# Rows of w and u as two bf16 parts, and column sums placed ahead of the rows, in an RWKV WKV kernel

## The chip, the cores and the metric

The kernel runs on one NeuronCore of a Trainium2 chip. The metric is the device time of one execution in microseconds (us): the median of seven runs for the kernel before. The core has a matrix engine (TensorE, PE in the profile, with its loads of weights shown as PEld), a vector engine (VectorE, DVE), an activation engine (ScalarE, ACT), a general engine (GpSimd, POOL), a queue engine that here issues most transfers (SyncE, SP), and 16 DMA engines that move data between device memory and on-chip memory. The engines run at the same time, each in its own program order, and wait for each other through semaphores.

## The reference

For 16 batches, 2048 time steps and 256 channels, a decayed softmax-like average of v runs over time. It keeps a numerator `aa`, a denominator `bb` and a running maximum `pp` for stability:

```
for t in range(seq_len):
    ww = u + kk                       # the current step, with bonus u
    qq = max(pp, ww)
    e1, e2 = exp(pp - qq), exp(ww - qq)
    output[b, t] = (e1 * aa + e2 * vv) / (e1 * bb + e2 + 1e-08)
    ww = pp - w + kk                  # as the reference has it; w is the decay
    qq = max(ww, kk)
    e1, e2 = exp(ww - qq), exp(kk - qq)
    aa, bb, pp = e1 * aa + e2 * vv, e1 * bb + e2, qq
```

All inputs and the output are float32. k, v and the output are 33.55 MB each; w and u are one row of 256 numbers (1 KB) each.

## The kernel before

**Tiles and slots.** Time is cut into 16 stretches of 128 steps, and the batches into 4 groups of 4. A tile n (there are NP = 64, with n = 4c + p for stretch c and group p) holds 128 time steps on the partitions and 4 batches times 256 channels along the free side: 128 x 1024 numbers, 512 KB in float32. The main loop handles one tile in each slot n. The first ten slots (LAG = 10, line 416) only take in tiles; from slot 10 on (line 437) a slot also finishes the output of tile n - 10 in its denominators and n - 11 in its numerators; a last loop (line 478) works off the 11 outputs that are left.

**What happens to one tile.** `load_k` and `load_v` (lines 61 and 65) bring k and v in; six buffers for k, five for v. `round_k` (line 173) copies k into the fp32r type on DVE. `logs` (line 178) makes the exponents in PSUM on PE in two kinds of matmuls: *rows* (line 184), four matmuls of 32 partitions each, which sit side by side in the array and multiply a coefficient matrix CO (time positions) with a matrix WU that holds w and u as rows, and *steps* (line 189), four matmuls of 128 partitions that add k with the matrices NLE and NLZ. `exps` (line 197) takes exponentials on ACT into a bf16 ring EZR. `times_v` (line 218) multiplies them by v on DVE. `sums` (line 237) adds up each tile's exponentials over time, eight narrow matmuls with 32 output columns each, into a bank MISC for the state that passes from one stretch of 128 steps to the next. `den` and `num` (lines 346 and 360) are the prefix sums of denominators and numerators on PE; `recip` (line 352) makes 1/denominator on ACT as a logarithm (line 355) and an exponential (line 357); `mult` (line 364) multiplies numerator by reciprocal on DVE; `store` (line 368) writes the output.

**The state.** After every fourth tile a chain of small work carries the state on: `copy_sums` (ACT, line 249), `turn` (PE), `state_logs` (ACT), `state_frames`, `state_scan` and `state_offsets` (POOL and DVE, lines 271 to 291), `state_weights` (ACT), `state_chain` (DVE), `turn_back` (PE), `inject` (DVE and DMAs of POOL) and `state_next` (POOL). A table `plan` (line 382) says in which slot, and at which named place of it, each part is issued. `state_offsets` runs on DVE for stretches 0, 1 and 15 and on POOL for the others.

**What sets the order.** Every instruction goes through `K`, which keeps the program's order on its engine. So the order of the calls in a slot is the order on each engine. PE's order in a slot from 10 on is: num of one half, den, `turn_back` if it is due, sums of the tile before (in even slots), num of the other half, rows and steps of the next tile, sums of the tile before (in odd slots), `turn` if it is due. ACT's order is: exponentials, logarithm, exponential of the reciprocal, with small work between. DVE's is: mult, `round_k` of tile n + 2, cast of v, mult, times_v. The numerators share one PSUM bank (NUMB), so the second num waits for the first mult; the denominators share one pair of banks (DENB), so a den waits for the logarithm that reads the one before; and the exponents of tile n + 1 use the banks that the exponentials of tile n have read (from slot 10 on, `half`, line 166).

**The queue of transfers.** SyncE issues nearly all loads and stores in program order. In a slot it issues the load of k of tile n + 6, a load of v, and the store of tile n - 11. In slots from 10 on, every fourth v goes through a POOL transfer that writes bf16.

**The start.** w and u are brought in by two small transfers of ACT's queue into `wuf` (lines 99 to 110); ACT copies `wuf` into WU in fp32r (line 412); the first rows follow. Ten matmuls of zeros (`idle_matmuls`, line 410) keep PE running meanwhile.

Of the kernel before, what the change touches and what calls it, by code (L numbers as in the profile page):

```python
# [7 lines left out]
F32 = mybir.dt.float32  # L8
F32R = mybir.dt.float32r
BF16 = mybir.dt.bfloat16  # L10
ALU = mybir.AluOpType
ACT = mybir.ActivationFunctionType
# [3 lines left out]
def kernel(  # L16
# [9 lines left out]
    K = tc.keep_in_program_order  # L26
    PE, DVE, SC, POOL, SP = nc.tensor, nc.vector, nc.scalar, nc.gpsimd, nc.sync

    B, T, Dm = k.shape
    HS = 64  # L30
    TC = 2 * HS
    NST = T // TC
    D = 2 * Dm
    NP = 4 * NST
    RING = 12
    AHEAD = 6
# [5 lines left out]
    consts = ctx.enter_context(tc.tile_pool(name="consts", bufs=1))  # L42
# [18 lines left out]
    def load_k(n, queue=SP):  # L61
        kr_of[n] = kpool.tile([128, 4, Dm], F32, tag="kr", name="kr")
        K(queue.dma_start(out=kr_of[n], in_=rows_of(k, n)))

    def load_v(n, queue=SP):
        if v_mode(n) == "dma":
            VB[n] = vbpool.tile([128, 4, Dm], BF16, tag="vb", name="vb")
            K(POOL.dma_start(out=VB[n], in_=rows_of(v, n)))
        else:
            vr_of[n] = vpool.tile([128, 4, Dm], F32, tag="vr", name="vr")  # L70
            K(queue.dma_start(out=vr_of[n], in_=rows_of(v, n)))
# [9 lines left out]
    def matrix(name, dt):  # L81
        return consts.tile([128, 128], dt, tag=name, name=name)

    def fill(ap, value):
        K(DVE.memset(ap.bitcast(F32) if ap.dtype == F32R else ap, value))

    GE, NE = ALU.is_ge, ALU.not_equal

    def select(ap, cmp, fill, base, cm, pattern):
        K(POOL.affine_select(out=ap, in_=ap, pattern=pattern, compare_op=cmp,  # L90
                             fill=fill, base=base, channel_multiplier=cm))

    M1, I1, Lx, COf = [matrix(x, F32) for x in ("M1", "I1", "Lx", "COf")]
    wuf = consts.tile([128, 2, Dm], F32, tag="wuf", name="wuf")
    CB_of = [consts.tile([128, 4, 128], BF16, tag=f"CB{j}", name=f"CB{j}") for j in range(2)]
    idle = CB_of[1].rearrange("p b x -> p (b x)")
    OH = consts.tile([128, 56], BF16, tag="OH", name="OH")
    Sel = consts.tile([128, 3, 2, 2, 4, 2], F32, tag="Sel", name="Sel")
    def load_row(eng, r, g0, x):
        K(eng.dma_start(out=wuf.rearrange("(g r) n d -> r g n d", r=32)[r, g0:4], in_=bass.AP(  # L100
            tensor=x.tensor, offset=x.offset, ap=[[0, 4 - g0], [0, 2], list(x.ap[0])])))

    K(POOL.memset(wuf[:, 0], 0.0))
    fill(wuf[:, 1], 0.0)
    fill(idle, 0.0)
    fill(M1, -1.0)
    fill(I1, 0.0)
    load_k(0)
    load_row(SC, 0, 0, w)
    load_row(SC, 1, 2, u)  # L110
    for n in range(1, AHEAD):
        load_k(n)
        load_v(n - 1)
    K(SC.preload_act_table_set("natural_log_exp_and_others"))
# [2 lines left out]
                    allow_small_or_imprecise_dtypes=True))  # L117
    select(M1, GE, 0.0, -1, -1, [[1, 128]])
    select(I1, NE, 1.0, 0, -1, [[1, 128]])
    for g in (2, 3):  # L120
        select(COf, NE, 1.0, -32 * g - 1, 1, [[0, 128]])

    NLE, NLZ, CO = matrix("NLE", F32R), matrix("NLZ", F32R), matrix("CO", F32R)
    K(DVE.tensor_scalar(NLE, M1, 0.5, None, ALU.add))
    for h in range(2):
        fill(NLE[HS * h:HS * h + HS, HS * (1 - h):HS * (2 - h)], 0.0)
    K(DVE.tensor_tensor(NLZ, NLE, I1, ALU.add))
    K(DVE.tensor_copy(CO, COf))  # L130
    fill(Lx, 1.0)
    fill(Sel, 0.0)
    fill(OH, 0.0)
    for h in range(2):
        fill(OH[HS * h:HS * h + HS, 24 + h:25 + h], 1.0)
        fill(OH[HS * h:HS * h + 1, 32 + h:33 + h], 1.0)
    for j, r in ((0, 0), (1, 8), (2, 64)):
        for h in range(2):
            select(Sel[:, j, h], NE, 1.0, -r - h, 1, [[-16, 2], [-2, 4], [-32, 2]])
    select(Lx, GE, 0.0, -1, -1, [[1, 128]])  # L140

    for h in range(2):
        select(Lx, NE, 1.0, -(HS * h + HS - 1), 1, [[0, 128]])
    WU = consts.tile([128, D], F32R, tag="WU", name="WU")
    mats = {"OH": OH, "Sel": Sel.rearrange("p a h n c i -> p (a h) n (c i)")}

    def out_matrices(*names):
# [18 lines left out]
    def half(n, z):  # L166
        j = (2 * n + z) % 3 if n < TURNS else z
        return PS[:, 2 * j:2 * j + 2, :]

    def ez(n):  # L170
        return EZR[:, :, n % RING]

    def round_k(n):
        km = consts.tile([128, 4, Dm], F32R, tag=f"km{n % 2}", name="km") if n < 2 else KM[n - 2]
        K(DVE.tensor_copy(km, kr_of.pop(n)))  # L175
        KM[n] = km

    def logs(n):
        km = KM[n].rearrange("p (i n) d -> p i (n d)", i=2)

        def rows(q):
            for i in range(2):
                g = 32 * (2 * q + i)
                K(PE.matmul(half(n, q)[:, i, :], CO[g:g + 32, :], WU[g:g + 32, :], start=True, stop=False,  # L184
                            tile_position=(g, 0), skip_group_check=True))

        def steps(q):
            for i in range(2):
                K(PE.matmul(half(n, q)[:, i, :], (NLE, NLZ)[q], km[:, i, :], start=False, stop=True,  # L189
                            skip_group_check=True))  # L190

        rows(0)
        rows(1)
        steps(0)
        steps(1)
# [41 lines left out]
    def sums(n):  # L237
        c, p = divmod(n, 4)
        t = MISC[:, 0:Dm]
        for o in range(2):  # L240
            x = 24 - 16 * o - 2 * p
            for j in range(4):
                q, i = divmod(j, 2)
                K(PE.matmul(t[32 * j:32 * j + 32, :], mats["OH"][:, x:x + 32],  # L244
                            ez(n)[:, 2 * q, i, Dm * o:Dm * o + Dm],
                            start=p == 0 and o == 0, stop=p == 3 and o == 1,
                            tile_position=(0, 32 * j), skip_group_check=True))
# [33 lines left out]

    def state_offsets(c):
        E = DVE if c in ON_DVE else POOL
        A, P, F = [x[c % 2] for x in (A_of, P_of, F_of)]
        out = A.rearrange("p h m -> p m h")
        Q = tiny.tile([128, 32, 2], F32, tag="Q", name="Q")
        K(E.tensor_tensor(Q, P[:, :, 0:2], F[:, :, 1:3], ALU.add))
        K(E.tensor_tensor(out[:, :, 0:2], Q, P[:, :, 1:3], ALU.subtract))
        K(E.tensor_single_scalar(out[:, :, 2:4], Q, CAP, op=ALU.min))
        K(E.tensor_single_scalar(out[:, :, 4:6], P[:, :, 1:3], -1.0, op=ALU.mult))  # L290
        K(E.tensor_copy(LL_of[(c + 1) % 2][:, 0, :, 0:1], P[:, :, 2:3]))

    def state_weights(c):
        G = tiny.tile([128, 6, 32], F32, tag="G", name="G")
# [57 lines left out]
    def recip(n, between=lambda: None):  # L352
        rd = rpool.tile([128, 2, D], F32, tag="rd", name="rd")
        for i in (slice(0, 1), slice(1, 2)) if n == NP - 1 else (slice(0, 2),):
            K(SC.activation(rd[:, i, :], DENB[:, i, :], ACT.Ln, scale=RS))  # L355
            between()
            K(SC.activation(rd[:, i, :], rd[:, i, :], ACT.Exp, scale=-1.0))  # L357
        RD[n] = rd

    def num(n, bank, i):  # L360
        for m, q in (("LN", 2), ("IdN", 3)):
            K(PE.matmul(bank, mats[m], ez(n)[:, q, i, :], start=q == 2, stop=q == 3, skip_group_check=True))  # L362

    def mult(n, bank, i):
        rd = RD[n]
        K(DVE.tensor_mul(rd[:, i, :], bank, rd[:, i, :]))  # L366
# [35 lines left out]
    def small_work(n, where):  # L402
        for f, c in later.pop((n, where), []):
            f(c)

    def idle_matmuls(n, bank):
        for _ in range(n):
            K(PE.matmul(bank, idle[:, 0:128], idle, start=True, stop=True, skip_group_check=True))

    idle_matmuls(10, MISC)  # L410
    round_k(0)
    K(SC.activation(WU, wuf.rearrange("p n d -> p (n d)"), ACT.Copy))  # L412
    logs(0)
    round_k(1)
    cast_v(0)
# [21 lines left out]
    for n in range(LAG, NP):  # L437

        q, qp = n - LAG, n - LAG - 1
        load(n + AHEAD)  # L440
        if qp >= 0:
            num(qp, NUMB, 0)
        den(q)
        small_work(n, "nums")

        if n % 2 == 0:
            sums(n - 1)
        exps(n)
        small_work(n, "act")
        recip(q, lambda: small_work(n, "recip"))  # L450
        if qp >= 0:
            mult(qp, NUMB, 0)
        small_work(n, "mid")
        if n + 2 < NP:
            round_k(n + 2)
        if n + 1 < NP:
            cast_v(n + 1)
        else:
            times_v(n)
        if qp >= 0:  # L460
            num(qp, NUMB, 1)
            mult(qp, NUMB, 1)
        small_work(n, "scan")
        if qp >= 0:
            store(qp)
        if n + 1 < NP:
            times_v(n)
            small_work(n, "chain")
            logs(n + 1)
        else:  # L470
            den(q + 1)
        if n % 2:
            sums(n - 1)
        small_work(n, "pe")
    sums(NP - 1)
    small_work(NP, "copy")
# [1 line left out]
    for n in range(NP, NP + LAG + 1):  # L478

        q, qp = n - LAG, n - LAG - 1  # L480
# [52 lines left out]
```

## Time and profile before

| | us |
|---|---|
| median of 7 runs (lowest to highest) | 292.58 (292.48 to 293.07) |
| profiled execution, its own time | 292.75 |
| its span | 291.04 |
| PE busy in the span | 269.8 (93%) |
| DVE busy | 256.7 (88%) |
| ACT busy | 257.1 (88%) |
| POOL busy | 118.5 (41%) |
| all 256 matmuls of the rows (line 184) | 33.8 |
| all 512 matmuls of the sums (line 244) | 25.6 |
| read from and written to device memory | 67.12 and 33.55 MB, 346 GB/s over the span |

The span is the stretch between the first and the last instruction that the profiler saw; the execution's own time has 1.71 us around it. Engine times overlap, so their shares don't add up to 100%. A matmul's duration contains its way through the array, and the next one starts before it ends; the distance of two starts tells more than a duration. The DMA share is the mean busy share of the 16 DMA engines; it can exceed 1, as packets of one engine overlap. In a timeline, "idle before <- releaser" is the time that the engine sat idle before an instruction, and what ended it. Where several instructions are merged, x tells how many.

### The profile page before, as it was taken

What the parts mean: (1) busy time and instruction counts of PE and PEld (TensorE: products, weight loads), DVE (VectorE), ACT (ScalarE), POOL (GpSimd) and SP (SyncE); (2) the same over time, 40 slices, a digit from 0 to 9 for tenths busy, and PEclk for the clock granted to TensorE, in tenths of its full rate; (3) what the DMA queues carried; (4) which work ended last, traced back from release to release, by engine and by line L of the source; (5) the groups of instructions that cost most, each with busy time, mean ns of one, the idle gap of its engine ahead of it and who ended that gap; (6) DMA issues with size and microseconds to landing.
All of it is one profiled execution on the core that took longest, in us unless ns stands there. A gap on an engine that the chain in (4) does not pass through costs nothing. (4 is left out here: it accounts for less than half of the span.)

```text
span 291.0 us, 4961 instructions
## 1 busy us (share of the span) xinstructions
PE 269.8 (93%) x1694; PEld 123.5 (42%) x1694; DVE 256.7 (88%) x441; ACT 257.1 (88%) x253; POOL 118.5 (41%) x219
## 2 busy tenths in 40 slices
PE   6799799999999999999999999999899999998881
PEld 1444354545344443544444443444354344434330
DVE  4399999999999989999999989998998989986753
ACT  1468579999999999999999999999899998999892
POOL 6000244354455555353445555353455545342200
PEclk9689999999999999999999999999999999999999
DMA  6999999999999999999999999999999999984686
GB/s 222 348 348 349 348 333 323 301 380 356 357 379 331 383 328 385 330 383 353 361 377 341 382 333 385 329 384 347 366 375 338 376 334 384 335 286 153 220 289 216
DMA packets 103516, 97.86 MB, mean 336 GB/s; under 512 B 4151, under 2 KB 103491, under 8 KB 103491
## 3 DMA queue, kind: packets, MB, share of 16 engines
q1 hardware_dynamic: 93744, 93.07, 94.7%
q0 software_dynamic: 9440, 4.20, 10.0%
q10 hardware_dynamic: 306, 0.27, 0.3%
q8 instruction: 13, 0.21, 0.3%
q14 instruction: 13, 0.10, 0.1%
HBM read 67.12 MB, written 33.55 MB: 346 GB/s over the span
## 5 line engine op out<-in xcount | busy, mean ns | idle before, releaser
L202 ACT ACTIVATE EZR<-PS 128x2048 bf16<-128x2048 f32 x54 | 100.9, 1868 | 5.3 <-PE PS L189 2.4
L366 DVE TENSOR_TENSOR rd<-PS,rd 128x512 f32<-128x512 f32 (+1 forms) x118 | 86.4, 734 | 13.0 <-PE PS L362 10.0
L220 DVE TENSOR_TENSOR EZR<-EZR,vb 128x2048 bf16<-128x2048 bf16 x64 | 77.5, 1211 | 4.8 <-ACT EZR L200 4.2
L339 POOL DMA_DIRECT2D EZR<-cb x64 | 38.5, 606 | 87.9 <-DVE cb L334 81.4
L357 ACT ACTIVATE rd<-rd 128x1024 f32<-128x1024 f32 (+1 forms) x65 | 68.0, 1046 | 1.2
L355 ACT ACTIVATE rd<-PS 128x1024 f32<-128x1024 f32 (+1 forms) x65 | 65.6, 1009 | 1.6 <-PE PS L349 1.5
L362 PE MATMUL PS<-EZR,LN 128*128 128x512 bf16 x128 | 49.1, 383 | 2.8 <-DVE rd L366 1.0
L175 DVE CAST km<-kr 128x1024 fp32r<-128x1024 f32 x64 | 44.7, 698 | 6.2 <-DMA kr<-in_k_dram 6.0
L189 PE MATMUL PS<-km,NLE 128*128 128x512 f32 x128 | 48.2, 459 | 1.2 <-DVE km L175 1.2
L362 PE MATMUL PS<-EZR,IdN 128*128 128x512 bf16 x128 | 48.4, 378 | 0.0
L189 PE MATMUL PS<-km,NLZ 128*128 128x512 f32 x128 | 41.0, 401 | 0.0
L349 PE MATMUL PS<-EZR,L 128*128 128x512 bf16 x128 | 38.0, 379 | 1.9 <-ACT rd L355 1.9
L349 PE MATMUL PS<-EZR,Id 128*128 128x512 bf16 x128 | 38.1, 379 | 0.0
L215 DVE CAST vb<-vr 128x1024 bf16<-128x1024 f32 x50 | 36.6, 732 | 0.9 <-DMA vr<-in_v_dram 0.9
L184 PE MATMUL PS<-WU,CO 32*128 32x512 f32 x256 | 33.8, 505 | 3.4 <-ACT WU L412 3.2
L275 POOL TENSOR_TENSOR F<-LL,LL 128x32 f32<-128x32 f32 x13 | 8.6, 662 | 50.5 <-ACT LL L266 50.5
L200 ACT ACTIVATE EZR<-PS 128x1024 bf16<-128x1024 f32 x20 | 19.4, 1021 | 9.2 <-PE PS L189 9.2
L189 PEld LDWEIGHTS PS<-km,NLZ 128*128 128x128 f32 x128 | 24.7, 193 | 6.2
L189 PEld LDWEIGHTS PS<-km,NLE 128*128 128x128 f32 x128 | 19.5, 192 | 17.4 <-issue 14.4
L184 PEld LDWEIGHTS PS<-WU,CO 32*128 32x128 f32 x256 | 12.9, 184 | 31.1 <-issue 13.8
L244 PE MATMUL PS<-EZR,OH 128*32 128x256 bf16 x512 | 25.6, 278 | 0.0
L362 PEld LDWEIGHTS <-LN 128*128 128x128 bf16 x128 | 12.7, 100 | 19.0 <-issue 15.0
(69 smaller groups left out, 219.4 us busy)
## 6 DMA issues: line engine op xcount, KB each, us to landing
kr<-in_k_dram SPq DMA_DIRECT2D x64, 512.0 KB, 9.0
out_dram<-rd SPq DMA_DIRECT2D x63, 512.0 KB, 8.2
vr<-in_v_dram SPq DMA_DIRECT2D x50, 512.0 KB, 9.0
vb<-in_v_dram POOLq DMA_DIRECT2D x14, 256.0 KB, 8.4
EZR<-cb POOLq DMA_DIRECT2D x64, 8.0 KB, 5.0
out_dram<-rd SPq DMA_DIRECT2D x2, 128.0 KB, 2.9
out_dram<-rd ACTq DMA_DIRECT2D x2, 128.0 KB, 3.2
wuf<-in_w_dram ACTq DMA_DIRECT2D x1, 8.0 KB
```

The source lines that it names most:

```text
L175: K(DVE.tensor_copy(km, kr_of.pop(n)))
L184: K(PE.matmul(half(n, q)[:, i, :], CO[g:g + 32, :], WU[g:g + 32, :], start=True, stop=False, tile_position=(g, 0), skip_group_check=True))
L189: K(PE.matmul(half(n, q)[:, i, :], (NLE, NLZ)[q], km[:, i, :], start=False, stop=True, skip_group_check=True))
L202: K(SC.activation(ez(n)[:, 0:2], PS[:, 0:4, :].rearrange("p (q i) x -> p q i x", q=2), ACT.Exp))
L215: K(DVE.tensor_copy(vb, vr))
L220: K(DVE.tensor_mul(ez(n)[:, 2:4], ez(n)[:, 0:2], vb.unsqueeze(1).broadcast_to([128, 2, 2, D])))
L339: K(POOL.dma_start(out=EZR[r:r + 1, 2 * q, r0:r0 + 4, :, :].rearrange("o p i (b x) -> o (p i b) x", b=4), in_=cb[x:x + 32, :]))
L349: K(PE.matmul(DENB[:, i, :], mats[m], ez(n)[:, q, i, :], start=q == 0, stop=q == 1, skip_group_check=True))
L355: K(SC.activation(rd[:, i, :], DENB[:, i, :], ACT.Ln, scale=RS))
L357: K(SC.activation(rd[:, i, :], rd[:, i, :], ACT.Exp, scale=-1.0))
L362: K(PE.matmul(bank, mats[m], ez(n)[:, q, i, :], start=q == 2, stop=q == 3, skip_group_check=True))
L366: K(DVE.tensor_mul(rd[:, i, :], bank, rd[:, i, :]))
```

## The change

- `wuf` becomes 128 x 256 instead of 128 x 2 x 256. Each row of w (u) is now written to two partitions, 16 apart, of every group of 32. From it comes WU in bf16 in two steps: ACT makes a bf16 copy WUH, then DVE computes WUH x Rest + wuf and rounds that to bf16. Rest is 0 on the first partition of a pair, so that it holds the row rounded to bf16, and -1 on the second, so that it holds what the rounding lost. Rest is made at the start by one select of POOL and one reduction of DVE. CO becomes bf16 and has its coefficients on both partitions, which takes four selects on POOL instead of two. The rows read WU twice along the free side (a broadcast) instead of reading two copies.
- The row of u is issued by SyncE, behind the loads of k(0) and k(1) and ahead of v(0); before, ACT's queue issued it behind w. The order of the other loads stays.
- From slot 10 on, the sums of the tile before are issued at one place in every slot: behind the second num and ahead of the rows. The call of `recip` moves to the same place in the text; it is ACT's alone, so ACT's order stays as it was, apart from the two small works that it calls between.
- In `state_offsets` the last two operations go to POOL for all stretches but the last; before, DVE had them for stretches 0 and 1.

```diff
-    wuf = consts.tile([128, 2, Dm], F32, tag="wuf", name="wuf")
+    wuf = consts.tile([128, Dm], F32, tag="wuf", name="wuf")
+    WUH = consts.tile([128, Dm], BF16, tag="WUH", name="WUH")
+    Rest4 = consts.tile([128, 4, 2], F32, tag="Rest4", name="Rest4")
+    Rest = consts.tile([128, 1], F32, tag="Rest", name="Rest")
...
     def load_row(eng, r, g0, x):
-        K(eng.dma_start(out=wuf.rearrange("(g r) n d -> r g n d", r=32)[r, g0:4], in_=bass.AP(
-            tensor=x.tensor, offset=x.offset, ap=[[0, 4 - g0], [0, 2], list(x.ap[0])])))
-
-    K(POOL.memset(wuf[:, 0], 0.0))
-    fill(wuf[:, 1], 0.0)
+        K(eng.dma_start(out=wuf.rearrange("(j r) d -> r j d", r=16)[r, 2 * g0:8], in_=bass.AP(
+            tensor=x.tensor, offset=x.offset, ap=[[0, 8 - 2 * g0], list(x.ap[0])])))
+
+    K(POOL.memset(wuf, 0.0))
...
     load_k(0)
     load_row(SC, 0, 0, w)
-    load_row(SC, 1, 2, u)
-    for n in range(1, AHEAD):
+    load_k(1)
+    load_row(SP, 1, 2, u)
+    load_v(0)
+    for n in range(2, AHEAD):
         load_k(n)
         load_v(n - 1)
...
-    for g in (2, 3):
-        select(COf, NE, 1.0, -32 * g - 1, 1, [[0, 128]])
+    for x in (65, 81, 97, 113):
+        select(COf, NE, 1.0, -x, 1, [[0, 128]])
...
-    NLE, NLZ, CO = matrix("NLE", F32R), matrix("NLZ", F32R), matrix("CO", F32R)
+    NLE, NLZ, CO = matrix("NLE", F32R), matrix("NLZ", F32R), matrix("CO", BF16)
...
+    fill(Rest4, 0.0)
...
+    select(Rest4, NE, -1.0, -16, 1, [[-32, 4], [-1, 2]])
...
-    WU = consts.tile([128, D], F32R, tag="WU", name="WU")
+    WU = consts.tile([128, Dm], BF16, tag="WU", name="WU")
...
-                K(PE.matmul(half(n, q)[:, i, :], CO[g:g + 32, :], WU[g:g + 32, :], start=True, stop=False,
+                K(PE.matmul(half(n, q)[:, i, :], CO[g:g + 32, :],
+                            WU[g:g + 32, :].unsqueeze(1).broadcast_to([32, 2, Dm]), start=True, stop=False,
                             tile_position=(g, 0), skip_group_check=True))
...
     def state_offsets(c):
         E = DVE if c in ON_DVE else POOL
+        E2 = POOL if c < NST - 1 else DVE
...
-        K(E.tensor_single_scalar(out[:, :, 4:6], P[:, :, 1:3], -1.0, op=ALU.mult))
-        K(E.tensor_copy(LL_of[(c + 1) % 2][:, 0, :, 0:1], P[:, :, 2:3]))
+        K(E2.tensor_single_scalar(out[:, :, 4:6], P[:, :, 1:3], -1.0, op=ALU.mult))
+        K(E2.tensor_copy(LL_of[(c + 1) % 2][:, 0, :, 0:1], P[:, :, 2:3]))
...
     idle_matmuls(10, MISC)
+    K(DVE.tensor_reduce(Rest, Rest4.rearrange("p g j -> p (g j)"), mybir.AxisListType.X, ALU.add))
     round_k(0)
-    K(SC.activation(WU, wuf.rearrange("p n d -> p (n d)"), ACT.Copy))
+    K(SC.activation(WUH, wuf, ACT.Copy))
+    K(DVE.scalar_tensor_tensor(WU, WUH, Rest, wuf, ALU.mult, ALU.add))
     logs(0)
...
         den(q)
         small_work(n, "nums")
-
-        if n % 2 == 0:
-            sums(n - 1)
         exps(n)
         small_work(n, "act")
-        recip(q, lambda: small_work(n, "recip"))
...
         if qp >= 0:
             num(qp, NUMB, 1)
+
+        sums(n - 1)
+        recip(q, lambda: small_work(n, "recip"))
+        if qp >= 0:
             mult(qp, NUMB, 1)
...
             den(q + 1)
-        if n % 2:
-            sums(n - 1)
         small_work(n, "pe")
     sums(NP - 1)
```

## The prediction

> **What bounds the kernel now.** I read four views: first the slices and stretches of the span, for the DMA share beside the engines; then the waits, split into two stretches; then the timeline of one late slot; last the drained end. The index n below is a slot (one pass of the loop, one tile of k and v); "rows", "steps" and "sums" are the matmuls of lines 184, 189 and 244.
>
> Stretches of the span (length, busy time of each engine, granted clock, DMA share, GB/s):
>
> ```profile
> 5.00:35.00 30.00, 24.87 (x153) 11.86 (x151) 23.42 (x49) 17.60 (x21) 1.41 (x4) 0.89 1.10 349
> 75.00:80.00 5.00, 4.77 (x34) 2.06 (x26) 4.54 (x11) 4.84 (x6) 1.48 (x4) 1.00 1.09 385
> 175.00:180.00 5.00, 4.76 (x32) 2.11 (x32) 4.93 (x11) 4.84 (x5) 2.44 (x4) 1.00 1.09 385
> 240.00:245.00 5.00, 4.41 (x26) 2.05 (x26) 4.93 (x11) 4.32 (x6) 1.52 (x3) 1.00 1.09 384
> 262.00:270.00 8.00, 7.03 (x50) 3.35 (x49) 5.07 (x17) 6.93 (x9) 1.57 (x4) 1.00 0.43 139
> ```
>
> The DMA share is 1.09 to 1.10 from 5 us to 245 us, and the rate does not move (349 GB/s while only loads run, 384 to 385 with stores among them) whether the engines are in their first, middle or late slots. It falls to 0.43 only after 262 us. So the transfers look full from the start until the last loads are in.
>
> The waits say from when the engines feel it. First DVE between 60 and 180 us, then DVE between 180 and 258 us (total us, times, longest):
>
> ```profile
> DVE rd L366 <- PE PS L362: 3.1, 8, 0.4
> DVE rd L366 <- issue: 2.3, 7, 0.3
> ```
>
> ```profile
> DVE km L175 <- DMA kr<-in_k_dram: 3.9, 10, 0.7
> DVE rd L366 <- PE PS L362: 1.0, 2, 0.7
> DVE rd L366 <- issue: 0.3, 1, 0.3
> ```
>
> Until 180 us no cast of k waits for its load; after that ten do. The two paces explain it. Engines: the exponentials of slot 16 start at 65.16 and those of slot 48 at 195.54, so 130.4 / 8 = 16.30 us for four slots. Loads: the casts of k(50) at 197.29 and k(62) at 248.05 each start as their load lands, so 50.76 / 3 = 16.92 us for four slots. The engines are the faster of the two; their cushion (the load of k(18) landed 4.6 us before its cast at 66.71) is used up near slot 48, and from there the loads set the time. At the engines' own pace slot 63 would start its exponentials at 65.16 + 47/4 x 16.30 = 256.7; it does so at 258.43. The SyncE queue, whose waits I read last, issues loads and stores in program order with no gap over 0.45 us until 262 us, so which bytes move before the last k is fixed by that order.
>
> Timeline of slot 62, from the last k on (start, us, engine, line):
>
> ```profile
> 252.21 0.69 DVE L175 CAST km<-kr 128x1024 fp32r<-128x1024 f32 x1 [0.33 <-DMA kr<-in_k_dram]
> ...
> 255.49 0.68 DVE L366 TENSOR_TENSOR rd<-PS,rd 128x512 f32<-128x512 f32 x1
> 255.75 0.40 PE L244 MATMUL PS<-EZR,OH 128*32 128x256 bf16 x8
> ...
> 256.22 0.38 PE L362 MATMUL PS<-EZR,LN 128*128 128x512 bf16 x1
> 256.44 0.38 PE L362 MATMUL PS<-EZR,IdN 128*128 128x512 bf16 x1
> 256.74 0.51 PE L184 MATMUL PS<-WU,CO 32*128 32x512 f32 x4
> 257.18 0.74 PE L189 MATMUL PS<-km,NLE 128*128 128x512 f32 x2
> 257.76 0.63 PE L189 MATMUL PS<-km,NLZ 128*128 128x512 f32 x2
> 258.43 1.88 ACT L202 ACTIVATE EZR<-PS 128x2048 bf16<-128x2048 f32 x1
> ...
> 262.23 0.62 PE L244 MATMUL PS<-EZR,OH 128*32 128x256 bf16 x16
> ```
>
> The last load lands at 252.2; DVE's orderly row of casts and products leads to the product at 255.49, that to num (256.22), rows, steps and the last exponentials. After that 11 outputs are worked off, and the end follows 32.6 us later.
>
> **The change, part by part.**
>
> *Start.* ACT's copy of the rows waits 4.11 us for u and starts at 8.44; rows start at 9.12. Now u is behind k(1) in SyncE's queue; k(1)'s cast starts at 6.60 as it lands, so u at about 6.6. Then an ACT copy of 128x256 (the copy of L254, same shape: 0.39) and one DVE operation of 128x256, which the trace lacks: between 0.29 (NLZ, 128x128) and 0.68 (mult, 128x512); I take 0.42, the copy of L252. Rows start near 6.6 + 0.39 + 0.42 + 0.1 for handing over = 7.5, 1.6 us earlier (1.3 to 1.75). u's issue costs SyncE some 0.53 ahead of v(0), which moves v(0) and all behind it from 1.82 to about 2.35. Cover: v(0)'s data can only follow k(1)'s, at 6.6; without that cover all loads, and the end, would be 0.5 later. Two more selects for CO and one for Rest (0.29 to 0.33 each) put POOL's Sel and Lx 1.0 us later, with first use at 18.08 for Lx; CO's cast and Rest on DVE lie in the 1.32 us that it waits for k(0). DVE's new operation delays the cast of k(1) from 6.6 to about 7.5, ahead of steps(1), at 12.47 now. All engine work before slot 48 has the same cover: the lead adds to a cushion that the loads eat. Price at the end: 0.
>
> [...]
>
> *Rows in bf16.* From rows to the first step 0.44 now (128.67 to 129.11 in slot 31). Streaming 512 columns takes 0.22 in either type (successive bf16 matmuls: 256.22, 256.44), so at most 0.22 can go and at least 0; the means differ by 0.08 (f32 0.459 against bf16 0.379) and loads of weights by 0.09. I take 0.08 less.
>
> *Sums ahead of rows.* From sums to the next matmul 0.34 (130.23 to 130.57). In odd slots sums ran behind the steps; now they stand in front of the rows: 0.34 - 0.08 = 0.26 later (0.12 to 0.34). In most even slots sums and num(1) only change places: 0. What queues behind: rows, steps, then ACT's exponentials. Over four middle slots: two odd ones pay 0.26, of which 0.11 each is slack (steps end at 122.04, exponentials start at 122.18); ACT's wait of 0.17 for POOL's A and 0.16 for PE in the even slots give some back. Net 2 x 0.15 - 0.33 = about 0, so 16.3 for four slots (16.30 + 2 x (0.12 - 0.11) - 0.33 = 16.0 to 16.30 + 2 x (0.34 - 0.11) = 16.8 with none given back). That is below the loads' 16.92, so: 0 at the end.
>
> The reciprocal only moves in the text; ACT's own order stays. The copy of the sums (L254) must now follow num(1): sums would end about 248.7, and it started at 248.78 behind the logarithm. 0.
>
> *Two offset operations to POOL for c = 0 and 1:* 0.44 + 0.22 on POOL for 0.22 + 0.18 on DVE, in slots 5 and 9; at most 0.4 on ACT's G there, covered by the cushion.
>
> *After the last load.* Here no cushion is left. In slot 62 the sums at 255.75 filled the time in which PE waited for the product at 255.49; behind num they are bare: exponentials 258.43 + 0.26 = 258.69. But at 262.23 sixteen sums (62 and 63) ran ahead of the next num at 262.78; only eight are left: 0.55 becomes 0.34, -0.21. What precedes them, den(54), waits for ACT's logarithm, +0.26. So num and all after: +0.05 (bounds: 0.12 - 0.21 = -0.09 and 0.34 - 0.21 = +0.13).
>
> Sum: span 291.04 + 0.05; around it the profiled execution has 292.75 - 291.04 = 1.71, together 292.80. The median is 292.58, 0.17 below this execution: **292.6**.
>
> [...] The rows show 385 at a full share. [...]
>
> **The rivals.**
>
> *The lead survives (faster).* If the share of 1.09 is not a limit, or loads queue only because stores and buffers hold them, an engine lead of 1.6 us passes to the last exponentials: 292.6 - 1.6 = 291.0, in part 291.0 to 292.0. For it: up to 180 us no cast waits for a load, and PE, ACT and DVE are all over 90% busy. Against: the constant rate, SyncE's queue without gaps, ten waits for k at the end.
>
> *Sums in front of the rows slow the engines past the loads (slower).* Place: odd slots, steps to exponentials. If the two odd slots pay 0.34 each, without slack and with nothing given back, four slots take 16.30 + 0.68 = 16.98. It decides from (258.69 - 63.56) / 11.75 = 16.61 on, 63.56 being slot 16 with the lead. Then slot 63 is at 63.56 + 11.75 x 16.98 = 263.1, +4.4: 297.0. For it: PE is 98% busy in the middle. Against: the slack above, and fewer changes between shapes of matmul on PE (three in a slot instead of four, each with a gap of about 0.09: 128.36 + 0.22 to 128.67).
>
> *The u row comes no sooner* (its queue makes it wait): no lead, same end, 292.6; it counts with the likeliest.
>
> **How the numbers follow.** 0.2% is 0.6 us here, about what a measurement of this kernel tells from no change. Likeliest (with the idle rival) 0.55: 292.6, own range 292.2 to 293.0 by the bounds above and 0.3 for the landing of the last load. Lead survives 0.24. Engines slowed 0.15. The rest, 0.06, is transfers themselves gaining or losing: 0.02 and 0.04 outside 0.2%. So faster 0.26, same 0.55, slower 0.19. The range takes in the faster rival and the near part of the slower: 291.0 to 293.8.
>
> **What would show it.** Rows first at about 7.5; the cast of the last k at 252.2 within 0.4; more than ten waits of km for its load, beginning before 180 us; last exponentials at 258.5 to 258.8; eight sums instead of sixteen near 262.5; DMA share unchanged. The lead survives if the last cast of k comes before 251. The slower rival holds if casts of k stop waiting and ACT waits for the steps in every odd slot.

## The result

| | before | after |
|---|---|---|
| median (lowest to highest), us | 292.74 (292.38 to 293.17), 33 runs | 293.73 (293.16 to 294.15), 13 runs |
| profiled execution: own time, span | 292.75, 291.04 | 293.61, 291.9 |
| cast of the last k starts | 252.21 | 253.05 |
| last exponentials start | 258.43 | 259.48 |
| from the last cast of k to the end | 38.83 | 38.85 |

The ratio is 1.0032 [1.0025, 1.0039]: the changed kernel is 0.3% slower. That is inside the range, 291.0 to 293.8, but outside the 0.2% that the likeliest case stood for and outside that case's own range, 292.2 to 293.0.

The page of the changed kernel, its first lines and the group of the rows (busy us, mean ns of one, then the idle time before them):

```profile
span 291.9 us, 4969 instructions
...
PE 263.6 (90%) x1694; PEld 120.1 (41%) x1694; DVE 256.1 (88%) x439; ACT 256.8 (88%) x253; POOL 122.2 (42%) x226
...
L191 PE MATMUL PS<-WU,CO 32*128 32x512 bf16 x256 | 26.5, 389 | 2.4 <-DVE WU L423 1.7
```

The rows cost PE 26.5 us instead of 33.8, and PE is busy for 6.2 us less. None of that reaches the end. The waits of DVE say why; first between 60 and 180 us, then between 180 and 258 us (total us, times, longest):

```profile
DVE km L182 <- DMA kr<-in_k_dram: 3.8, 9, 0.5
```

```profile
DVE km L182 <- DMA kr<-in_k_dram: 6.9, 14, 1.3
```

Casts of k now wait for their loads from the middle of the kernel on; before, none did until 180 us, and then ten, for 3.9 us. The engines became faster and wait more. The timeline of the changed kernel from the last k on:

```profile
253.05 0.69 DVE L182 CAST km<-kr 128x1024 fp32r<-128x1024 f32 x1 [0.52 <-DMA kr<-in_k_dram]
...
257.28 0.38 PE L371 MATMUL PS<-EZR,IdN 128*128 128x512 bf16 x1
257.58 0.40 PE L252 MATMUL PS<-EZR,OH 128*32 128x256 bf16 x8
257.92 0.39 PE L191 MATMUL PS<-WU,CO 32*128 32x512 bf16 x4
258.24 0.73 PE L197 MATMUL PS<-km,NLE 128*128 128x512 f32 x2
...
259.48 1.88 ACT L210 ACTIVATE EZR<-PS 128x2048 bf16<-128x2048 f32 x1
...
263.28 0.41 PE L252 MATMUL PS<-EZR,OH 128*32 128x256 bf16 x8
```

From the last cast to the last exponentials it takes 6.43 us, before 6.22: +0.21, as the sums now stand bare between num and rows (257.58 to 257.92). At 263.28 only eight sums are left, which gives it back: from the last cast to the end there are 38.85 us against 38.83. So nothing behind the last load got slower. Of the 0.86 us by which the profiled span is longer, 0.84 are there at 253.05: **the last load landed later**, though the same bytes go in the same order, but for the row of u. The stretch with loads and stores among each other shows it as a rate; first before, then after:

```profile
60.00:240.00 180.00, 176.30 (x1144) 80.85 (x1144) 170.01 (x275) 173.47 (x165) 87.99 (x154) 1.00 1.12 360
```

```profile
60.00:240.00 180.00, 170.70 (x1130) 79.08 (x1131) 168.69 (x274) 172.45 (x165) 88.68 (x153) 1.00 1.12 359
```

1 GB/s of 360 over 180 us is 0.5 us, at one and the same DMA share of 1.12. Counting data packets in the two traces gives the lag, that is, how much later the same number of packets is done in the changed kernel: 0.34 us at 6.2 us, 0.17 from 10 to 50 us, 0.25 at 60, 0.47 at 125, 0.7 at 240. A small step at the start, then a slow slip.

### The profile page after: what moved, and what is told of

Same layout as the page of the kernel before. It is cut to its first block, busy times and chain, and to the rows that moved or that the text cites. A ratio compares the mean times of both kernels' runs of the same rounds, so it can differ in the third digit from the quotient of the medians.

```text
span 291.9 us, 4969 instructions
## 1 busy us (share of the span) xinstructions
PE 263.6 (90%) x1694; PEld 120.1 (41%) x1694; DVE 256.1 (88%) x439; ACT 256.8 (88%) x253; POOL 122.2 (42%) x226
## 5 line engine op out<-in xcount | busy, mean ns | idle before, releaser
L182 DVE CAST km<-kr 128x1024 fp32r<-128x1024 f32 x64 | 45.5, 711 | 12.0 <-DMA kr<-in_k_dram 12.0
L197 PE MATMUL PS<-km,NLE 128*128 128x512 f32 x128 | 47.6, 454 | 3.1 <-DVE km L182 3.0
L223 DVE CAST vb<-vr 128x1024 bf16<-128x1024 f32 x50 | 36.0, 720 | 1.4 <-DMA vr<-in_v_dram 1.3
L191 PE MATMUL PS<-WU,CO 32*128 32x512 bf16 x256 | 26.5, 389 | 2.4 <-DVE WU L423 1.7
L371 PEld LDWEIGHTS <-IdN 128*128 128x128 bf16 x128 | 12.4, 97 | 26.3 <-issue 23.5
L296 POOL TENSOR_TENSOR Q<-P,F 128x64 f32<-128x64 f32 x13 | 15.7, 1204 | 11.3 <-DVE P L287 11.3
```

Of the source, the lines that this page charges most:

```text
L223: K(DVE.tensor_copy(vb, vr))
```

## The experiments

Ratios are against the kernel before, run on the same chip in the same rounds (its medians there lie between 292.72 and 292.77). "Last k" is the start of the last cast of k in the profiled run (252.21 before, 253.05 after).

| run | kernel | median, us | ratio | last k |
|---|---|---|---|---|
| e1 | after, row of u back on ACT's queue | 293.92 | 1.0035 [1.0021, 1.0049] | 253.33 |
| e2 | before, row of u on SyncE | 293.11 | 1.0011 [1.0002, 1.0020] | 252.72 |
| e3 | before, sums and reciprocal moved | 293.00 | 1.0006 [0.9997, 1.0016] | 252.15 |
| e4 | after, offset operations back on DVE | 293.62 | 1.0031 [1.0021, 1.0040] | 252.99 |
| e5 | after, 2240 B of padding: the old addresses | 292.99 | 1.0004 [0.9995, 1.0014] | 252.59 |
| e6 | before, 64 B of padding | 293.78 | 1.0032 [1.0019, 1.0044] | 253.11 |
| e7 | after, edits of e1 and e5 | 292.84 | 1.0001 [0.9993, 1.0010] | 252.30 |
| e8 | before, 384 B of padding | 290.42 | 0.9911 [0.9896, 0.9926] | 249.02 |
| e9 | before, 32 B of padding | 293.08 | 1.0011 [1.0003, 1.0020] | 252.56 |
| e10 | before, 64 B ahead of the output buffers | 292.77 | 1.0001 [0.9992, 1.0010] | 252.15 |
| e11 | before, k and v buffers alone moved by 64 B | 293.73 | 1.0032 [1.0020, 1.0044] | 252.90 |
| e12 | after, 2624 B of padding | 288.43 | 0.9851 [0.9835, 0.9867] | 248.25 |

**The start: e1, e2.** The row of u stands ahead of v(0) in SyncE's queue. SyncE's queue in the changed kernel (start, length of the issue, us):

```profile
1.84 0.66 SPq L104 DMA_DIRECT2D wuf<-in_u_dram  x1
2.55 0.40 SPq L71 DMA_DIRECT2D vr<-in_v_dram  x1
```

v(0) was issued at 1.82 before. Is that the loss? In e1 the changed kernel gets the old start, in e2 the old kernel the new one:

```diff
-    load_k(1)
-    load_row(SP, 1, 2, u)
-    load_v(0)
-    for n in range(2, AHEAD):
+    load_row(SC, 1, 2, u)
+    for n in range(1, AHEAD):
```

> The changed kernel with one part undone: the row of u goes back to ACT's queue, behind w, and SyncE issues k(0), k(1), v(0) without it. Theory S (start): SyncE's issue of u held v(0) back by 0.73 us (2.55 instead of 1.82), the DMA engines ran short near 6 us, and every later load is late by that; then the last cast of k comes back to about 252.2 from 253.05 and the time to 292.7 to 292.9 (ratio 0.999 to 1.001 to before), though the rows start near 9 again instead of 7.4. Rival M (middle): the transfers lose the most in the middle, where the engines now run ahead or the sums stand elsewhere; then only some 0.2 to 0.3 comes back, 293.3 to 293.5 (ratio 1.002 to 1.003). Rival P (POOL's two offset operations): no change, 293.7.

> The kernel before with this one part of the change: the row of u is issued by SyncE behind k(1) and ahead of v(0). Theory S: all of the loss comes with it, 293.3 to 293.7 (ratio 1.002 to 1.003), the last cast of k near 253, v(0) issued near 2.5. Rival M: 292.9 to 293.1 (ratio 1.0005 to 1.001). Rival P: as before, 292.7.

With the old start the loss stays, 1.0035, so the start isn't its cause: theory S fails. Alone, the new start costs the old kernel 1.0011, some 0.3 us.

**The sums and the offsets: e3, e4.** e3 makes only the third point of the change (sums at one place, `recip` behind it) in the old kernel; e4 takes back the fourth point, the two POOL operations of stretches 0 and 1, in the changed one. e4's edit:

```diff
-        E2 = POOL if c < NST - 1 else DVE
+        E2 = E
```

> The kernel before with this one part of the change: sums ahead of the rows in every slot (rows stay fp32r in one part, u stays on ACT's queue). Theory S: the loads are untouched, the last cast of k at 252.2; behind it the exponentials come 0.34 later and the sums of the drained end 0.21 sooner, so 292.8 to 292.9 (ratio 1.000 to 1.0006). Rival M: 293.1 to 293.3 (ratio 1.001 to 1.002), last cast of k at 252.6 or later. The slower rival of the prediction, engines past the loads: over 295.

> The changed kernel with the two offset operations of stretches 0 and 1 back on DVE. Theory S and rival M: no change, 293.7 (ratio to before 1.003). Rival P: POOL's operations hold back its transfers, and without them 0.3 us or more comes back, 293.4 or less.

Timeline of e3:

```profile
252.15 0.69 DVE L175 CAST km<-kr 128x1024 fp32r<-128x1024 f32 x1 [0.37 <-DMA kr<-in_k_dram]
...
258.68 1.88 ACT L202 ACTIVATE EZR<-PS 128x2048 bf16<-128x2048 f32 x1 [0.24 <-PE PS L189]
```

The last load is where it was; the exponentials are 0.25 later and wait for the steps. Counted from the last cast they come after 6.53 us instead of 6.22: +0.31, where e3's own expectation had 0.34. (The prediction's +0.26 has 0.08 taken off for bf16 rows, and e3's rows are still fp32r.) From there to the end it takes 32.38 us instead of 32.61: -0.23, for the prediction's -0.21. The span is 291.06 against 291.04. e4 leaves the loss as it is, so these two operations aren't in it.

**The addresses: e5, e6, e7.** What was left is a thing that no line of the diff names. The constants come first in a partition's memory, and WU (2048 to 512 B), `wuf` (2048 to 1024), CO (512 to 256) and the new WUH, Rest4 and Rest change their total by -2240 B. Every buffer behind them moves: in the built programs the buffers of k and v start 128 B past a multiple of 512 B before, and 448 B past one after. (The addresses are those that the program assigns; the trace doesn't show them.) A tile that nothing uses, behind WU, sets them at will: 2240 B in the changed kernel for the old addresses, 64 B in the old kernel for the same place within 256 B as in the changed one (192 B past a multiple). The edit of e5 (e6 has 16 numbers in place of 560):

```diff
     WU = ...
+    pad = consts.tile([128, 560], F32, tag="pad", name="pad")
```

> The changed kernel with an unused tile of 2240 bytes behind WU, so that the ring, the k, v and output buffers lie at the same addresses of a partition as in the kernel before (128 past a multiple of 512 bytes; in the changed kernel 448 past, which is 64 past a multiple of 128). Theory A (addresses): the DMA engines are a little slower on the shifted rows, about 0.3% over the 250 us of loads; the padded kernel keeps the loss of 0.3 to 0.4 at the start alone, 293.0 to 293.2 (ratio 1.001 to 1.0015). Rival F (flow): the loss in the middle comes from what the engines do, since they reach the pace of the loads earlier; then padding changes nothing, 293.6 to 293.9 (ratio 1.003). Rival S alone: 293.7 too.

> The kernel before, nothing changed but an unused tile of 64 bytes behind WU, which shifts every buffer behind it to 64 past a multiple of 128 bytes. Theory A: slower by 0.5 to 1.0 us, 293.3 to 293.8 (ratio 1.002 to 1.0035), with the last cast of k near 253. Rival F: no change, 292.7 (ratio 1.000).

> The changed kernel with both: the 2240 bytes of padding and the row of u on ACT's queue again. Theory A with theory S: both losses are gone, 292.4 to 292.8 (ratio 0.999 to 1.000), last cast of k at 252.2 or a little before. Rival F: 293.7 to 293.9 (ratio 1.003), as with u on ACT alone.

Timeline of e6, the old kernel with 64 unused bytes:

```profile
253.11 0.69 DVE L176 CAST km<-kr 128x1024 fp32r<-128x1024 f32 x1 [0.40 <-DMA kr<-in_k_dram]
...
259.33 1.88 ACT L203 ACTIVATE EZR<-PS 128x2048 bf16<-128x2048 f32 x1
```

The last cast of k, first in e5, then in e7:

```profile
252.59 0.69 DVE L183 CAST km<-kr 128x1024 fp32r<-128x1024 f32 x1 [0.38 <-DMA kr<-in_k_dram]
```

```profile
252.30 0.69 DVE L181 CAST km<-kr 128x1024 fp32r<-128x1024 f32 x1 [0.39 <-DMA kr<-in_k_dram]
```

The padding alone makes the last load land 0.9 us later and the time 1.0032, the same as the whole change; its chain from load to exponentials is the old 6.22. Put back to the old addresses, the changed kernel is at 1.0004. This is the cause. The start adds little to it: e5's last k is still 0.38 late, and with the old start as well (e7) 0.09, but the medians of e5 and e7 differ by 0.15 us only, and their intervals overlap. So e5 came out a little below the 1.001 to 1.0015 expected of it.

**Which buffers, and which offsets: e8 to e11.** e8 puts all buffers on multiples of 512 B (a padding of 96 numbers in the old kernel), e9 moves them by 32 B (8 numbers). e10 moves only what lies from the output buffers on, whose bytes the stores read (`gap1` ahead of their pool); e11 moves k's and v's alone (what lies behind them moves by 512 B, which keeps its place within 512 B):

```diff
+    gap1 = ctx.enter_context(tc.tile_pool(name="gap1", bufs=1))
+    gap1.tile([128, 16], F32, tag="gap1", name="gap1")
     kpool = ...
     vpool = ...
+    gap2 = ctx.enter_context(tc.tile_pool(name="gap2", bufs=1))
+    gap2.tile([128, 112], F32, tag="gap2", name="gap2")
     vbpool = ...
```

> The kernel before with 384 unused bytes behind WU: the ring and all buffers start at a multiple of 512 bytes of a partition instead of 128 past one. If only the place within 128 bytes counts: no change, 292.7 (ratio 1.000). If larger steps count too (512): faster, 292.4 or less (ratio 0.999 or less).

> The kernel before with 32 unused bytes behind WU: every buffer 32 past a multiple of 128 (and of 64). If the DMA engines cut their accesses at multiples of 64 bytes: slower than the shift by 64, over 293.8 (ratio over 1.0035). If at 128: like it, 293.6 to 293.9 (ratio 1.003).

> The kernel before with 64 unused bytes ahead of the output buffers (rd) alone: k, v and the ring keep their places. If what costs is the reads of the stores from on-chip memory: most of the loss, ratio 1.002 to 1.0035. If it is the writes of the loads: none, ratio 1.000.

> The kernel before with 64 unused bytes ahead of the buffers of k and v, and 448 behind them, so that these alone lie 64 past a multiple of 128. If what costs is the writes of the loads: most of the loss, ratio 1.002 to 1.0035. If it is the reads of the stores: none, ratio 1.000.

The last cast of k, first in e10, then in e11:

```profile
252.15 0.69 DVE L177 CAST km<-kr 128x1024 fp32r<-128x1024 f32 x1 [0.39 <-DMA kr<-in_k_dram]
```

```profile
252.90 0.69 DVE L179 CAST km<-kr 128x1024 fp32r<-128x1024 f32 x1 [0.42 <-DMA kr<-in_k_dram]
```

So it is the loads' writes into the buffers of k and v (e11, 1.0032), not the stores' reads (e10, 1.0001). Nor is it the engines: e11 leaves the ring EZR where it was, and the casts that read k's buffers take 0.70 us on average there as before. But the loss doesn't come at the start, while only loads run. There e6 has the rate of before, 349 GB/s:

```profile
5.00:35.00 30.00, 25.00 (x153) 11.85 (x151) 23.48 (x49) 17.70 (x21) 1.36 (x4) 0.89 1.09 349
```

By the count of packets e6 is 0.1 us ahead of the kernel before until 40 us and 0.6 behind at 250; e11 is 0.2 ahead until 50 us and 0.4 behind at 250. The loads fall behind only later, with stores among them.

e9 fits neither of its expectations: 32 B cost about a third of what 64 B cost (1.0011 against 1.0032, though the ends of the intervals meet, at 1.0020). Stretches of e8, while only loads run and later, then its last k:

```profile
5.00:35.00 30.00, 25.43 (x157) 11.97 (x161) 24.04 (x50) 18.28 (x22) 2.10 (x5) 0.89 1.09 384
75.00:80.00 5.00, 4.62 (x26) 2.36 (x27) 4.88 (x11) 4.82 (x6) 1.52 (x3) 1.00 1.09 385
```

```profile
249.02 0.68 DVE L176 CAST km<-kr 128x1024 fp32r<-128x1024 f32 x1
...
255.51 1.88 ACT L203 ACTIVATE EZR<-PS 128x2048 bf16<-128x2048 f32 x1
```

On multiples of 512 B loads alone run at 384 GB/s instead of 349, at a DMA share of 1.09 against 1.10. By the count of packets they are some 5 us ahead at 60 us and stay so. The last cast of k waits for nothing: the engines set the end, and slot 16 to slot 63 at their pace of 16.26 us for four slots, (194.55 - 64.44) / 8, give it (64.44 + 11.75 x 16.26 = 255.5, measured 255.51). That is the pace of before, 16.30, so the engines gained next to nothing from the addresses. The profiled run is one of the two fastest of six (289.53; the six lie from 289.22 to 290.65).

By the place of the buffers past a multiple of 256 B the ratios go 0.9911 at 0 (e8), 1 at 128 (before), 1.0011 at 160 (e9), 1.0032 at 192 (after, e6, e11). The rate while only loads run doesn't follow that order: it is 384 GB/s in e8 and 349 before, but e6 still has 349 between 5 and 35 us, the changed kernel 349 between 10 and 35 us. Nor did the stores' reads show a cost in e10 (1.0001). So the runs put the places in order; by what mechanism, they don't show. The row of the changed kernel:

```profile
10.00:35.00 25.00, 21.73 (x140) 9.82 (x138) 21.41 (x44) 15.39 (x19) 0.91 (x3) 0.81 1.09 349
```

**Both together: e12.** The changed kernel with its buffers on multiples of 512 B (2624 B of padding).

> The changed kernel with 2624 unused bytes behind WU, so that its ring and buffers start at the same addresses as in the kernel shifted by 384: multiples of 512 bytes. There (290.42) no cast of k after 60 us waited for its load, so the engines set the time. In the changed kernel, where nothing waited (slots 16 to 32), four slots took (128.47 - 65.25) / 4 = 15.8 us instead of 16.3. If the rest of the change is a gain that the loads have hidden: the engines gain until the loads bind again at their 16.9 us for four slots, the casts of k wait at the end again, the last exponentials start near 253.7 instead of 255.5, and the time is 288 to 289.5 (ratio 0.984 to 0.989), below both kernels and the shifted one. If the change is worth nothing by itself: 290.4 (ratio 0.991). If it costs something by itself (the sums in front of the rows, the start of v(0)): over 290.8 (ratio over 0.993).

Its waits of DVE from 60 to 258 us, and its last k:

```profile
DVE km L183 <- DMA kr<-in_k_dram: 7.1, 16, 1.0
```

```profile
248.25 0.69 DVE L183 CAST km<-kr 128x1024 fp32r<-128x1024 f32 x1 [0.42 <-DMA kr<-in_k_dram]
...
254.69 1.88 ACT L211 ACTIVATE EZR<-PS 128x2048 bf16<-128x2048 f32 x1
```

At 288.43 us it beats both kernels. Once the loads leave room, the change is worth some 0.6% (0.9851 / 0.9911 = 0.994; the medians of e8 and e12 are 2.0 us apart, the profiled runs 1.0, and all four runs of e12 are faster than all six of e8). Then its casts of k run into the loads again, 4.8 us earlier than in the changed kernel. The last exponentials came at 254.69, not near 253.7 as expected.

## Why the prediction was right or wrong

*What bounds the kernel.* Right: the loads set the last slots, and faster engines ahead of them change nothing. e5 is the change without its side effect, 1.0004: "no change", as forecast, once the addresses are the old ones. But "the transfers look full" was read too far. For the same loads a DMA share of 1.10 stood beside 349 GB/s (before) and 1.09 beside 384 (e8); it says that packets were under way, not how fast one is. (The reading of SyncE's queue was off by a little too: between 1 and 246 us its longest gap is 0.49, at 84.44. Nothing rests on it.)

*The step that failed:* "so which bytes move before the last k is fixed by that order", and from it the cast of the last k "at 252.2 within 0.4". The order fixes the bytes, not the time that they take. That time hangs on where the buffers lie, and the change moved them by 2240 B without a line that says so. The prediction gave transfers "gaining or losing" 0.06 in all, without a mechanism. Measured: +0.84 us in the profile after, +0.90 in e6 from the address alone. With that the last exponentials came at 259.48, outside the 258.5 to 258.8 that was to show the prediction right. That the time still lies in the stated range is luck: its upper end, 293.8, was there for engines that fall behind the loads, and they didn't.

*The start.* Rows start at 7.40 (forecast 7.5), by an ACT copy of 0.42 (0.39) and a DVE operation of 0.48 (0.42):

```profile
6.41 0.42 ACT L422 ACTIVATE WUH<-wuf 128x256 bf16<-128x256 f32 x1 [2.78 <-DMA wuf<-in_u_dram]
6.86 0.48 DVE L423 SCALAR_TENSOR_TENSOR WU<-WUH,Rest,wuf 128x256 bf16<-128x256 bf16 x1 [1.24 <-ACT WUH L422]
7.40 0.40 PE L191 MATMUL PS<-WU,CO 32*128 32x512 bf16 x4 [1.70 <-DVE WU L423]
```

The lead was eaten, but neither where nor only by what the prediction named (a cushion until slot 48). At the first exponentials of slot 5 it had grown to 3.1 us (21.57 against 24.70 before). The gap on PE ahead of the first rows had 1.70 us instead of 3.15, and the granted clock between 10 and 20 us was 0.86 instead of 0.67. That the clock follows from the gap was not shown: e1 has 3.2 us of gap, and a clock of 0.70 between 10 and 15 us and 1.00 between 15 and 20. Then the engines met the loads, early:

```profile
24.09 0.69 DVE L182 CAST km<-kr 128x1024 fp32r<-128x1024 f32 x1 [1.06 <-DMA kr<-in_k_dram]
...
24.84 0.73 PE L197 MATMUL PS<-km,NLE 128*128 128x512 f32 x2 [1.67 <-DVE km L182]
```

```profile
25.00:30.00 5.00, 3.68 (x20) 1.68 (x21) 4.28 (x11) 2.30 (x3) 0.63 (x2) 0.65 1.09 350
```

PE stood idle for 1.67 us waiting for k, the granted clock between 25 and 30 us was 0.65 (1.00 before), and at the exponentials of slot 16 nothing of the lead was left: 65.25 against 65.16. How much of it the wait took and how much the clock was not separated. In e12, with the loads at 384 GB/s, the cast of that k doesn't wait, the clock stays at 1.00, and slot 16 starts at 62.98.

The cover named for u's issue, that v(0)'s data can only follow k(1)'s, held only in part: v(0) came at 2.55 instead of 2.35 (issue 0.66, not 0.53), and between 5 and 10 us the loads had less to do, 326 GB/s at 1.07 in the changed kernel against 350 at 1.10 before (and 350 at 1.09 in e1, with the old start):

```profile
5.00:10.00 5.00, 2.98 (x14) 1.07 (x12) 2.40 (x4) 1.93 (x3) 1.75 (x6) 0.94 1.07 326
```

```profile
5.00:10.00 5.00, 1.85 (x8) 0.59 (x7) 2.08 (x3) 0.63 (x1) 1.16 (x3) 0.98 1.10 350
```

The price of 0 should have been 0 to 0.5, and e2 measures 0.3 (0.1 to 0.6 by its interval). In the changed kernel the same edit shows nothing (e1), so this term doesn't simply add; why stays open.

*Rows and sums.* Behind num in the last slot, from start to start (a bf16 matmul of 512 columns lasts 0.38 us there, and the next starts 0.22 after it, 257.06 and 257.28), sums to rows took 0.34 (forecast 0.34) and rows to steps 0.32 instead of 0.44: 0.12 less (0.08). Hence +0.21 for +0.26, and 38.85 against 38.83 behind the last load for +0.05. For the pace of four slots the forecast was 16.3, at best 16.0. Starts of the exponentials, eight slots apart and ahead of the waits for loads, give 65.25 to 96.87 in the changed kernel: 15.8. The same for e3 gives 56.97 to 88.95: 16.0. So the move of the sums alone brought 0.3 for a forecast of "about 0", and the rest of the change, the bf16 rows above all, another 0.2. The size was off on the good side; a possible reason, fewer changes of shape on PE, stood in the text only as an argument against a rival and wasn't tried by itself. Against loads at 16.9 it brought nothing; it counts in e12, where slots also pass at 15.8 (55.17 to 86.77 for eight).

*The rivals.* "The lead survives" fell: more casts wait for loads than before. "Sums slow the engines" fell: 15.8 us for four slots, not 16.98. The rival in which the row of u comes no sooner fell: rows started at 7.40, before at 9.12. The case that came true, slower by a mechanism in the transfers, held 0.04.

*Still open:* by what mechanism the place of a target changes the time of a load; why 32 B cost less than 64 B; why the 64 B cost only with stores among the loads (349 for 349 without), while the gain of multiples of 512 B shows only while loads run alone (384 for 349) and not with stores among them (385 for 385). Moving the buffers of k alone or of v alone, moving these two alone to multiples of 512 B (e8 moves all buffers), and multiples of 256 B that aren't multiples of 512 B weren't tried.

## What to carry to other kernels

When a change adds, drops or resizes a tile, list the addresses of the buffers behind it before pricing its work: an unused tile that restores them separates the change from its side effect in one run. Try the targets of large loads on round addresses (here multiples of 512 B) first, then tune the engines; here that was worth 0.9% by itself, and on top of it the change that had lost 0.3% gains some 0.6%. Transfers that look always busy are a bound only at the rate they have been measured at: here a share of 1.10 stood beside 349 GB/s before, and 1.09 beside 384 in e8.

## What was not expected of the hardware

- The place of a load's target within the partition changed its rate: while only loads run (5 to 35 us) 349 GB/s with targets 128 B past a multiple of 512 B, 384 on the multiple (e8), at DMA shares of 1.10 and 1.09.
- 64 B more cost 0.32% of the kernel (e6, e11), 32 B 0.11% (e9); the same 64 B under the stores' source cost nothing (1.0001, e10). The 64 B don't show in the loads-only rate (349 in e6); the loads fall behind only with stores among them.
- A transfer of 4 KB (the row of u) held SyncE's queue for 0.66 us (0.68 in e2), longer than the first loads of 512 KB beside it (0.40 to 0.51).
